# Units of last-stage weights in the mLSTM stage: a fixed step for each load and each split

## The chip, the cores and the metric

One core of one Trainium2 chip runs the whole kernel in one launch. The metric is the device time of an execution in microseconds, median over several runs. The profile is of one further execution on the chip.

## What is computed

Two decoder layers on a sequence of 2048 tokens of width 1024, each `x <- x + mixer(rmsnorm(x))`, and a last norm. The first mixer is an mLSTM (4 heads, per head 512 value and 256 key columns), the second an RG-LRU with block-diagonal gates. The reference, cut to the part in which the change lies, and to where the weights of the last stage are used:

```python
q = jnp.einsum('bshd,hde->bhse', xch, w_q).astype(jnp.float32) * (M_DK ** -0.5)
k = jnp.einsum('bshd,hde->bhse', xch, w_k).astype(jnp.float32)
v = jnp.einsum('bshd,hde->bhse', xmh, w_v).astype(jnp.float32)
...
def step(carry, inp):                       # over chunks of the sequence
    ...
    Sm = jnp.einsum('bhtk,bhsk->bhts', qb, kb) * W
    num = (decay[..., None] * jnp.einsum('bhtk,bhkv->bhtv', qb, C)
           + jnp.einsum('bhts,bhsv->bhtv', Sm, vb))
    ...
    C_new = d_last[..., None, None] * C + jnp.einsum('bhs,bhsk,bhsv->bhkv', w_last, kb, vb)
...
r = jax.nn.sigmoid(jnp.einsum('bsnc,ncd->bsnd', xb, w_a).reshape(bsz, s, R_WIDTH) + b_a)
ig = jax.nn.sigmoid(jnp.einsum('bsnc,ncd->bsnd', xb, w_x).reshape(bsz, s, R_WIDTH) + b_x)
...
return y @ w_out
```

## The kernel before

Every float32 operand of a matmul is split in two parts: `hi`, a cast to float32r on ScalarE (ACT, L759), and `lo = x - hi` on VectorE (DVE, L762). A product is three matmuls (`mm3`, L359 to L361): hi by hi, hi by lo, lo by hi. So weights cost a load, a cast and a subtraction before TensorE (PE) can use them.

The stages run one after the other: `phase_a1` (input projection), `phase_a2` (the mLSTM stage), `phase_b1` (output projection and the second layer's input projection) and `phase_b2` (gates, scan, output projection, last norm).

In `phase_a2` a loop runs over 32 blocks (h, b): 4 heads by 8 blocks of 256 tokens, each of two chunks c of 128. One pass, here a step, does the recurrence of block (h, b) and the projections of the block after it. In program order: `norm` of the block before, `loads` (xc, xm, sz, o and the rows qb and db of the next block, through the queue of SP), `recur` for chunk 0, `finish` of the block before (transposes `pt`, `y`, its write through the queue of GpSimd, POOL), `qk` (q and k of the next block), `recur` for chunk 1, `score`, and `value` for both chunks. `value` projects v and evicts it from PSUM: `vh` by ACT (L954), `vl` by DVE (L955). `recur` makes `kv` for two halves m of the state, adds it to the states `C0` and `C1` on DVE (L986) and splits these to `Ch` and `Cl`; there is one `kv` bank pair, so the second half's matmuls wait for DVE to read the first. It also makes the numerator `n`, which `hh` reads (L1009); there is one `n`, too. Mean and variance `mv` (L1017) go to POOL (`frs`, L1022 to L1025), then ACT normalizes `hh` (L1029).

The stage also prepares weights in two ways, through one pool `wraw` of two buffers:

- `head_weights` loads and splits the q, k and v weights of a head. The call for q stands in step b = 3 and that for k in b = 5 of the head before; v is called for in `qk` of a head's block 0, that is in step 7 of the head before, and has one pair of buffers.
- `later_weights` is a generator of 20 units for `phase_b2`: 8 of gate weights (128 x 768, written to `d_gw`) and 12 of output weights (128 x 1024, to `d_ow`). A unit takes both buffers: it loads `raw`, casts it to `hi` and subtracts in place, and POOL writes both parts to DRAM. Five units are called for in each head, at b = 1, 2, 4, 6 and 7.

Where an instruction ends up in its engine's queue is not decided by the place of the call: a scheduler lays the queues out, taking instructions as their inputs and buffers come free, and each engine then works through its queue in order. The method `order(first, then)` (L765) adds a constraint without a semaphore: an instruction of `then` stands behind those of `first` on the same engine. In this stage it is used for the first head only before the change (L820 to L823, L876 and L889). `split_into` (L756) returns the cast and the subtraction.

Of the kernel before, what the change touches and what calls it, by code (L numbers as in the profile page):

```python
# [7 lines left out]
F32 = mybir.dt.float32  # L8
F32R = mybir.dt.float32r
I32 = mybir.dt.int32  # L10
AF = mybir.ActivationFunctionType
ALU = mybir.AluOpType
# [9 lines left out]
H = 4  # L22
DV = 512
# [283 lines left out]
class Trunk:  # L307
# [465 lines left out]
    def phase_a2(self, wq, wk, wv, rgate, rwout, D):  # L773
        tc, nc = self.tc, self.nc
        BL = 256
        NB = T // BL
        with ExitStack() as ctx:
# [12 lines left out]
            vh = [va.tile([P, 516], F32R, name=f"vh{i}") for i in range(NVA)]  # L790
            vl = [va.tile([P, 516], F32R, name=f"vl{i}") for i in range(NVA)]
# [10 lines left out]
            def head_weights(h, names):  # L802
                w = W.setdefault(h, {})
                for nm in names:
                    src = {"q": wq[h], "k": wk[h], "v0": wv[h, :, :, 0:256], "v1": wv[h, :, :, 256:512]}[nm]
                    raw = wp.tile([P, KV, 256], F32, tag="wraw", name="wraw", bufs=2)
                    nc.sync.dma_start(raw, src)
                    if nm[0] == "v":
                        j = int(nm[1])
                        if j == 0:  # L810
                            w["v"] = (wp.tile([P, KV, 512], F32R, tag="vwh", name="vwh"),
                                      wp.tile([P, KV, 512], F32R, tag="vwl", name="vwl"))
                        hi, lo = (t[:, :, j * 256:(j + 1) * 256] for t in w["v"])
                    else:
                        pool = ob if h % 2 else wp
                        w[nm] = (pool.tile([P, KV, 256], F32R, tag=nm + "wh", name=nm + "wh"),
                                 pool.tile([P, KV, 256], F32R, tag=nm + "wl", name=nm + "wl"))
                        hi, lo = w[nm]
                    a = self.split_into(hi, lo, raw, "a", "v")
                    if h == 0 and nm[0] == "v":  # L820
                        self.order((self.kT,), a)
                    if h == 0 and nm in "qk":
                        self.order(a, self.tail[-4:])  # L823

            def later_weights():

                parts = [(rgate[i // 2, :, i % 2 * 768:(i % 2 + 1) * 768],
                          [D["gw"][i, :, l * 768:(l + 1) * 768] for l in range(2)]) for i in range(8)]
                parts += [(rwout[k], [D["ow"].rearrange("(h k) p (l n) -> k l p h n", h=2, l=2)[k, l] for l in range(2)])
                          for k in range(12)]  # L830
                for src, keep in parts:
                    n = src.shape[-1]
                    raw, hi = (wp.tile([P, KV * 256], F32, tag="wraw", name="wraw", bufs=2)[:, 0:n] for _ in range(2))
                    nc.sync.dma_start(raw, src)
                    self.split_into(hi.bitcast(F32R), raw.bitcast(F32R), raw, "a", "v")
                    for t, k in zip((hi, raw), keep):
                        nc.gpsimd.dma_start(k, t if n == 768 else t.rearrange("p (h n) -> p h n", h=2))
                    yield

            def project(h, b):  # L840
# [14 lines left out]
                def loads():  # L855
                    if (h, b) != (0, 0):
                        rows()
                    if (h, b) == (0, 0):
                        head_weights(h, ("q", "k"))
                    xm = lp.tile([P, KV, BL], F32, tag="xm", name="xm")  # L860
                    xc = lp.tile([P, KV, BL], F32, tag="xc", name="xc")
                    nc.sync.dma_start(xc, D["xc"][hs, :, bs].rearrange("k p t -> p k t"))
                    nc.sync.dma_start(xm, D["xm"][hs, :, bs].rearrange("k p t -> p k t"))
                    if (h, b) == (0, 0):
                        rows()
                    S["sz"] = sz = lp.tile([P, KV, BL], F32, tag="sz", name="sz")
                    S["o"] = o = lp.tile([P, 2, DV], F32, tag="o", name="o")
                    nc.sync.dma_start(sz, D["sz"][hs, :, bs].rearrange("k p t -> p k t"))
                    nc.sync.dma_start(o, D["o"][b * 2:b * 2 + 2, :, h * DV:(h + 1) * DV].rearrange("c p n -> p c n"))
                    for nm, x in (("xc", xc), ("xm", xm)):  # L870
                        hi = xp.tile([P, KV, BL], F32R, tag=nm + "h", name=nm + "h")
                        lo = xp.tile([P, KV, BL], F32R, tag=nm + "l", name=nm + "l")
                        fi = (h, b, nm) == (0, 0, "xc")
                        a = self.split_into(hi, lo, x, "v" if fi else "a", "v")
                        if fi:
                            self.order(a, self.tail[-4:])  # L876
                        S[nm] = (hi, lo)
                    S["xcf"] = xc
# [66 lines left out]
                def value(c):  # L945
                    xh, xl = S["xm"]
                    wh, wl = W[h]["v"]
                    ps = pr.tile([P, DV], F32, tag="r", name="pj")
                    for k in range(KV):
                        cs = slice(c * P, (c + 1) * P)  # L950
                        self.mm3(ps, xh[:, k, cs], xl[:, k, cs], wh[:, k], wl[:, k], k == 0, k == KV - 1)
                    i = (b * 2 + c) % NVA
                    p2 = ps.rearrange("p (a b) -> p a b", a=2)
                    nc.scalar.copy(halves(vh[i]), p2)  # L954
                    nc.vector.tensor_tensor(halves(vl[i]), p2, halves(vh[i]).bitcast(F32), op=ALU.subtract)  # L955

                return S, [loads, qk, score, lambda: value(0), lambda: value(1)]

# [93 lines left out]
            later = later_weights()  # L1052
# [6 lines left out]
            for i, (h, b) in enumerate(blocks):  # L1059
                if i + 1 < len(blocks):  # L1060
                    Sn, (loads, qk, score, v0, v1) = project(*blocks[i + 1])
                else:
                    Sn, loads = None, lambda: None
                    qk = score = v0 = v1 = loads
                if late:
                    norm(*late)
                loads()
                recur(h, b, 0, S)
                if late:
                    finish(*late)  # L1070
                qk()
                recur(h, b, 1, S)
                score()
                v0()
                v1()
                if b in (3, 5) and h < H - 1:
                    head_weights(h + 1, "q" if b == 3 else "k")
                elif b in (1, 2, 4, 6, 7):
                    next(later, None)
                late = (h, b, S)  # L1080
                S = Sn
            norm(*late)
# [571 lines left out]
```

## Time and profile before

| | us |
|---|---|
| median of 3 runs | 3015.86 (3013.2 to 3016.79) |
| the profiled execution | 3013.4 |
| its span, first to last instruction | 3011.5 |
| PE busy | 2868.1 (95% of the span) |
| DVE busy | 2126.0 (71%) |
| ACT busy | 1515.3 (50%) |
| POOL busy | 456.2 (15%) |
| value evictions by ACT (`vh`, L954), first and last start | 1015.4, 1726.5 |

Times in the profile's rows count from the start of the span. A row of the timeline has start, length, engine, line, operation, out<-in, shapes and, in brackets, how long the engine was idle before and what it waited for. The granted clock of PE is a share of its full speed. The value evictions mark the steps of the mLSTM stage, and the stage lasts from about 1005 to about 1745 us.

### The profile page before, as it was taken

The page shows a single profiled execution, that of the slowest core. Times are in us where ns is not written, and L with a number is a line of the kernel's source. Part 1 is how long each engine was busy: PE and PEld are TensorE (multiplying, and loading weights), DVE is VectorE, ACT ScalarE, POOL GpSimd, SP SyncE. Part 2 cuts the span into 40 slices and gives each one's busy share as a digit, 9 for nine tenths or more (in the row PEclk, how much of TensorE's full clock was granted, in tenths as well). Part 3 has the DMA queues.
Part 4 walks back from the last instruction along what each step waited for, and adds up shares of the span by engine and source line. Part 5 has one row for each costly group of instructions (what it writes and reads, how often), then busy time and mean ns, then how long its engine had stood idle before and what let it go on. Part 6 is the DMA issues. An engine that isn't in the chain of part 4 may idle for free. (4 is left out here: it accounts for less than half of the span.)

```text
span 3011.5 us, 43205 instructions
## 1 busy us (share of the span) xinstructions
PE 2868.1 (95%) x15442; PEld 2455.6 (82%) x15442; DVE 2126.0 (71%) x3584; ACT 1515.3 (50%) x2545; POOL 456.2 (15%) x846
## 2 busy tenths in 40 slices
PE   7999999999999899898998979999999999899997
PEld 5799987899987798897988968787788887678885
DVE  7766798536577587787777855677888566666763
ACT  6344555324345566566665633434434322976761
POOL 1211122102123111112112111101221111000000
PEclk9999999999999999999999989999999999999998
DMA  6767677668889754546455467776776665878855
GB/s 229 270 219 248 231 253 242 216 208 307 273 309 301 232 167 160 191 143 218 157 181 183 148 237 256 264 231 202 259 241 227 212 198 181 307 256 300 295 196 171
DMA packets 294839, 686.58 MB, mean 228 GB/s; under 512 B 29024, under 2 KB 107616, under 8 KB 294624
## 3 DMA queue, kind: packets, MB, share of 16 engines
q1 hardware_dynamic: 227440, 450.34, 47.0%
q0 software_dynamic: 66608, 232.43, 20.3%
q8 instruction: 121, 1.98, 0.3%
q10 hardware_dynamic: 576, 1.05, 0.1%
q14 instruction: 94, 0.77, 0.1%
HBM read 446.53 MB, written 237.17 MB: 227 GB/s over the span
## 5 line engine op out<-in xcount | busy, mean ns | idle before, releaser
L759 ACT CAST s<-raw 128x512 fp32r<-128x512 f32 (+1 forms) x280 | 172.1, 620 | 259.9 <-PE pd L361 69.3
L762 DVE TENSOR_TENSOR s<-raw,s 128x512 fp32r<-128x512 f32 (+1 forms) x280 | 191.6, 689 | 64.1 <-ACT s L759 63.1
L359 PE MATMUL acc<-yh,wr 128*128 128x512 f32 x384 | 151.2, 402 | 17.1 <-DMA wr<-d_ow 8.3
L360 PE MATMUL acc<-yl,wr 128*128 128x512 f32 x384 | 153.0, 398 | 0.6 <-DVE yl L762 0.6
L361 PE MATMUL acc<-yh,wr 128*128 128x512 f32 x384 | 152.6, 398 | 0.0
L759 ACT CAST u<-t 128x512 fp32r<-128x512 f32 x112 | 68.8, 619 | 154.1 <-PE pc L361 51.0
L686 DVE SCALAR_TENSOR_TENSOR xc<-xm,vec,xc 128x512 f32<-128x512 f32 x192 | 139.2, 746 | 5.8 <-ACT xc L684 4.4
L762 DVE TENSOR_TENSOR u<-t,u 128x512 fp32r<-128x512 f32 x112 | 76.7, 690 | 84.8 <-ACT u L759 84.3
L759 ACT CAST s<-sum 128x512 fp32r<-128x512 f32 (+1 forms) x120 | 74.1, 618 | 115.8 <-PE pc L361 44.3
L359 PE MATMUL pa<-u,s 128*128 128x512 f32 x304 | 122.1, 402 | 4.6 <-ACT p L258 3.1
L360 PE MATMUL pa<-u,s 128*128 128x512 f32 x304 | 121.4, 399 | 0.0
L361 PE MATMUL pa<-u,s 128*128 128x512 f32 x304 | 121.3, 400 | 0.1
L686 DVE SCALAR_TENSOR_TENSOR xc<-xr,vec,xc 128x512 f32<-128x512 f32 x144 | 106.0, 748 | 9.2 <-ACT xc L684 7.9
L986 DVE SCALAR_TENSOR_TENSOR C<-C,dl,kv 128x516 f32<-128x516 f32 x112 | 83.6, 746 | 39.8 <-PE kv L361 39.8
L759 ACT CAST Ch<-C 128x516 fp32r<-128x516 f32 x120 | 74.7, 623 | 65.9 <-DVE da L1004 52.5
L359 PEld LDWEIGHTS acc<-yh,wr 128*128 128x128 f32 x384 | 72.7, 191 | 38.1 <-issue 8.7
L359 PE MATMUL pj<-vwh,xmh 128*128 128x512 f32 x256 | 102.7, 402 | 0.3 <-ACT vwh L759 0.3
L360 PE MATMUL pj<-vwl,xmh 128*128 128x512 f32 x256 | 99.8, 390 | 0.7 <-DVE vwl L762 0.7
L762 DVE TENSOR_TENSOR s<-sum,s 128x512 fp32r<-128x512 f32 (+1 forms) x120 | 82.6, 689 | 25.0 <-ACT s L759 24.0
L361 PE MATMUL pj<-vwh,xml 128*128 128x512 f32 x256 | 100.1, 391 | 0.0
L359 PE MATMUL kv<-vh,kh 128*128 128x258 f32 x240 | 73.8, 307 | 26.4 <-ACT vh L954 15.3
L360 PE MATMUL pd<-u,s 128*128 128x512 f32 x224 | 88.5, 395 | 1.6 <-DVE u L762 1.6
(479 smaller groups left out, 10089.2 us busy)
## 6 DMA issues: line engine op xcount, KB each, us to landing
wr<-d_ow SPq DMA_DIRECT2D x96, 512.0 KB, 4.4
d_wx<-s POOLq DMA_DIRECT2D x64, 512.0 KB, 4.3
s<-d_wx SPq DMA_DIRECT2D x64, 512.0 KB, 4.4
s<-d_ws SPq DMA_DIRECT2D x64, 512.0 KB, 6.2
raw<-in_wxz_dram SPq DMA_DIRECT2D x124, 256.0 KB, 4.8
d_wr<-s POOLq DMA_DIRECT2D x48, 512.0 KB, 3.7
s<-d_wr SPq DMA_DIRECT2D x48, 512.0 KB, 4.2
wg<-d_gw SPq DMA_DIRECT2D x32, 768.0 KB, 5.0
```

Source lines behind the costliest of these rows:

```text
L359: mm(out, sh, mh, start=first, stop=False, skip_group_check=resumed)
L360: mm(out, sh, ml, start=False, stop=False, skip_group_check=resumed)
L361: mm(out, sl, mh, start=False, stop=last, skip_group_check=resumed)
L686: nc.vector.scalar_tensor_tensor(out, x[:, j:j + TB], self.v(wn, m * 4 + j), out, op0=ALU.mult, op1=ALU.add)
L759: a = nc.scalar.copy(hi, src)
L762: b = (nc.gpsimd if lo_eng == "p" else nc.vector).tensor_tensor(lo, src, hi.bitcast(F32), op=ALU.subtract)
L986: nc.vector.scalar_tensor_tensor(C2, C2, self.dl[:, r:r + 1], p2, op0=ALU.mult, op1=ALU.add)
```

## The change

Three things, all in `phase_a2`. The q and k weights of the next head are called for in steps 0 and 1 instead of 3 and 5, and their splits stand behind `self.valued`, the last value eviction (ACT behind ACT, DVE behind DVE). The units are cut in two: the load, issued from a step's start and put behind `self.loaded`, the load of `o` of that step, and the split with its writes, called for at the step's end and put behind `self.valued`. And the units have other steps: b = 2 to 6 in head 0, 2 to 5 in heads 1 and 2, 0 to 6 in head 3.

```diff
                     a = self.split_into(hi, lo, raw, "a", "v")
                     if h == 0 and nm[0] == "v":
                         self.order((self.kT,), a)
-                    if h == 0 and nm in "qk":
-                        self.order(a, self.tail[-4:])
+                    if nm in "qk":
+                        if h == 0:
+                            self.order(a, self.tail[-4:])
+                        else:
+                            self.order(self.valued, a)
...
-                    nc.sync.dma_start(raw, src)
-                    self.split_into(hi.bitcast(F32R), raw.bitcast(F32R), raw, "a", "v")
+                    self.order(self.loaded, (nc.sync.dma_start(raw, src),))
+                    yield
+                    a, v = self.split_into(hi.bitcast(F32R), raw.bitcast(F32R), raw, "a", "v")
+                    self.order(self.valued, (a, v))
                     for t, k in zip((hi, raw), keep):
                         nc.gpsimd.dma_start(k, t if n == 768 else t.rearrange("p (h n) -> p h n", h=2))
                     yield
...
-                    nc.sync.dma_start(o, D["o"][b * 2:b * 2 + 2, :, h * DV:(h + 1) * DV].rearrange("c p n -> p c n"))
+                    self.loaded = (nc.sync.dma_start(o, D["o"][b * 2:b * 2 + 2, :, h * DV:(h + 1) * DV].rearrange("c p n -> p c n")),)
...
-                    nc.scalar.copy(halves(vh[i]), p2)
-                    nc.vector.tensor_tensor(halves(vl[i]), p2, halves(vh[i]).bitcast(F32), op=ALU.subtract)
+                    self.valued = (nc.scalar.copy(halves(vh[i]), p2),
+                                   nc.vector.tensor_tensor(halves(vl[i]), p2, halves(vh[i]).bitcast(F32),
+                                                           op=ALU.subtract))
...
                 loads()
+                extra = b < 7 if h == H - 1 else 2 <= b <= 5 + (h == 0)
+                if extra:
+                    next(later, None)
                 recur(h, b, 0, S)
...
                 v1()
-                if b in (3, 5) and h < H - 1:
-                    head_weights(h + 1, "q" if b == 3 else "k")
-                elif b in (1, 2, 4, 6, 7):
+                if extra:
                     next(later, None)
+                if b < 2 and h < H - 1:
+                    head_weights(h + 1, "qk"[b])
```

The built programs show what the scheduler makes of it. The order of every engine is the same in both outside this stage. First the queue of SP in head 1 (`in_rgate` is a unit's load, `in_wq` that of q weights; the other rows are loads of a step). Before:

```order
L834 DMA wraw_12863<-in_rgate_dram 128x768
L851 DMA qb_13152<-d_q_88 128x256
L869 DMA o_12338<-d_o_80 128x2x512
L834 DMA wraw_13143<-in_rgate_dram 128x768
L863 DMA xm_12876<-d_xm_81 128x4x256
L862 DMA xc_12877<-d_xc_82 128x4x256
L868 DMA sz_12337<-d_sz_83 128x4x256
L853 DMA db_12873<-d_dec_89 128x256
L807 DMA wraw_13423<-in_wq_dram 128x1024
L834 DMA wraw_13702<-in_rgate_dram 128x768
```

and after:

```order
L874 DMA o_12886<-d_o_80 128x2x512
L837 DMA wraw_12897<-in_rgate_dram 128x768
L868 DMA xm_13441<-d_xm_81 128x4x256
L873 DMA sz_12885<-d_sz_83 128x4x256
L858 DMA db_13438<-d_dec_89 128x256
L867 DMA xc_13442<-d_xc_82 128x4x256
L856 DMA qb_13997<-d_q_88 128x256
L874 DMA o_13166<-d_o_80 128x2x512
L868 DMA xm_13721<-d_xm_81 128x4x256
L837 DMA wraw_13177<-in_rgate_dram 128x768
```

Before, four loads into `wraw` stand within one step's loads, in the first steps of the head; after, there is one to a step, behind that step's `o`, and SP's loads of a step run about one step ahead of its work.

Second, the queue of DVE at the start of a step in head 2, behind the eviction of block 4's second chunk (`C0`, `C1` are the state's halves, `y` the output of the block before). Before:

```order
L955 TENSOR_TENSOR vl3_9957<-pj_15335,vh3_9953 128x2x256
L762 TENSOR_TENSOR xml_15376<-xm_15363,xmh_15375 128x1024
L762 TENSOR_TENSOR Cl0_15389<-C0_14564,Ch0_15388 128x516
L986 SCALAR_TENSOR_TENSOR C1_14583<-C1_14583,dl_77,kv_15404 128x516
L1004 TENSOR_SCALAR da_15422<-n_15379 128x1
L1005 SCALAR_TENSOR_TENSOR da_15422<-n_15379,da_15422,enT_76 128x1
L1007 RECIPROCAL da_15422<-da_15422 128x1
L1009 SCALAR_TENSOR_TENSOR hh_15426<-n_15379,da_15422,o_15088 128x512
L762 TENSOR_TENSOR Cl1_15413<-C1_14583,Ch1_15412 128x516
L1016 BN_STATS st_15429<-hh_15426 128x6
L1046 TENSOR_TENSOR y_15432<-y_15432,skx_14956 128x1024
```

and after:

```order
L960 TENSOR_TENSOR vl3_9957<-pj_15336,vh3_9953 128x2x256
L762 TENSOR_TENSOR xml_15374<-xm_15361,xmh_15373 128x1024
L762 TENSOR_TENSOR wraw_15097<-wraw_15097,wraw_15098 128x1024
L762 TENSOR_TENSOR Cl0_15390<-C0_14557,Ch0_15389 128x516
L992 SCALAR_TENSOR_TENSOR C1_14576<-C1_14576,dl_77,kv_15405 128x516
L1010 TENSOR_SCALAR da_15423<-n_15380 128x1
L1052 TENSOR_TENSOR y_15433<-y_15433,skx_14955 128x1024
L762 TENSOR_TENSOR Cl1_15414<-C1_14576,Ch1_15413 128x516
L1011 SCALAR_TENSOR_TENSOR da_15423<-n_15380,da_15423,enT_76 128x1
L1054 TENSOR_TENSOR y_15433<-y_15433,sz_14806 128x1024
L1013 RECIPROCAL da_15423<-da_15423 128x1
L908 SCALAR_TENSOR_TENSOR qd_15484<-pj_15457,db_15358 128x512
```

A unit's subtraction now stands third in the step, behind the eviction and `xml`; in the step before the change there is no `wraw` row at all. `hh` falls behind both `y`. A few rows further, in both, comes `C0` of the second chunk and then `xcl`; the rows ahead of that `C0` are the same but for the unit's and for `mv`, which follows it after the change.

Third, ACT at the end of the stage, from the last value eviction on (`t30`, `t31` are the first loads of `phase_b1`, `u220` to `u223` their parts). Before:

```order
L954 CAST vh3_9953<-pj_18648 128x2x256
L759 CAST Ch0_18681<-C0_16771 128x516
L759 CAST u220_18855<-t30_18827 128x512
L759 CAST u221_18858<-t30_18827 128x512
L759 CAST Ch1_18705<-C1_16790 128x516
L1042 ACTIVATE y_18725<-pt_18726,vec_58 128x256
L759 CAST u223_18899<-t31_18829 128x512
L759 CAST u222_18861<-t31_18829 128x512
```

and after:

```order
L959 CAST vh3_9953<-pj_18658 128x2x256
L759 CAST wraw_18420<-wraw_18419 128x1024
L759 CAST Ch0_18688<-C0_16760 128x516
L1048 ACTIVATE y_18732<-pt_18733,vec_58 128x256 x2
L759 CAST Ch1_18712<-C1_16779 128x516
L1048 ACTIVATE y_18732<-pt_18740,vec_58 128x256 x2
L759 CAST u220_18855<-t30_18827 128x512
L759 CAST u221_18858<-t30_18827 128x512
L759 CAST u223_18899<-t31_18829 128x512
L759 CAST u222_18861<-t31_18829 128x512
L1035 ACTIVATE hh_18726<-hh_18726,frs_18778 128x512
```

The last unit's cast follows the last eviction. The tiles `t30` and `t31` lie in the memory of the two `wraw` buffers: their loads wait for that unit's writes now, where they waited for a unit written some five steps earlier. The `u` casts moved together, ahead of the last norm of `hh`.

## The prediction

> **What bounds the kernel now.** The change touches only the mLSTM stage, so I cut that stage by its steps. A step here runs from one start of the second value cast (L954, the `vh` of a block's second chunk) to the next; step (h, b) is the pass of the loop for head h and block b. First view: busy time by stretch (us from the start, its length, then PE, PEld, DVE, ACT and POOL busy with counts, the granted clock, the DMA share, GB/s). The stretches are steps (0,0) to (0,2), (0,7) to (1,2), (1,3) to (1,6), (1,7) to (2,2) and (2,7) to (3,2).
>
> ```profile
> 1019.30:1088.10 68.80, 61.98 (x430) 57.61 (x429) 55.31 (x100) 42.04 (x77) 13.22 (x27) 0.98 0.62 204
> 1172.40:1274.00 101.60, 87.45 (x583) 80.44 (x582) 75.50 (x133) 59.57 (x112) 17.99 (x34) 0.93 0.61 197
> 1274.00:1358.10 84.10, 83.58 (x615) 79.05 (x614) 69.39 (x128) 53.61 (x105) 10.21 (x24) 1.00 0.43 138
> 1358.10:1457.90 99.80, 86.36 (x584) 80.56 (x583) 76.37 (x133) 61.14 (x112) 21.29 (x34) 0.93 0.65 216
> 1542.00:1644.00 102.00, 86.96 (x579) 80.55 (x578) 75.17 (x132) 60.15 (x111) 22.57 (x36) 0.92 0.62 206
> ```
>
> In the third row PE is busy 83.58 of 84.10 us at clock 1.00: four steps of 84.10 / 4 = **21.03 us**, bound by TensorE. The four steps around each change of head take 101.60, 99.80 and 102.00 us, with 13 to 15 us of PE idle and a lower clock. Against 84.10 that is 17.5 + 15.7 + 17.9 = 51.1 us; the first three steps are 68.80 - 3 x 21.03 = 5.7 us over. So **56.8 us** of excess lie in 15 steps.
>
> The same view for the tile `wraw` alone (DVE, ACT, POOL busy) says where the splits run:
>
> ```profile
> 1172.40:1274.00 101.60, 9.83 (x9) 8.58 (x9) 6.16 (x10) 0.93 0.61 197
> 1274.00:1358.10 84.10, 0.00 (x0) 0.00 (x0) 0.00 (x0) 1.00 0.43 138
> ```
>
> All nine of that head are in the rough stretch, none in the quiet one. The waits of PE, and then of ACT, between 1019.3 and 1726.5 (total us, times, longest):
>
> ```profile
> PE pt L1039 <- ACT hh L1029: 15.5, 9, 6.4
> PE kv L359 <- ACT vh L954: 15.0, 5, 4.5
> PE kv L359 <- DVE C L986: 10.3, 11, 2.9
> ```
> ```profile
> ACT wraw L759 <- DMA wraw<-in_rwout_dram: 15.9, 6, 5.1
> ...
> ACT wraw L759 <- DMA wraw<-in_rgate_dram: 10.4, 4, 6.5
> ```
>
> PE waits for things that ACT does late, and ACT is late because it stands at a split whose weights have not landed. One such place in the timeline (start, length, in brackets the idle time before it):
>
> ```profile
> 1374.29 0.34 SPq L834 DMA_DIRECT2D wraw<-in_rwout_dram  x1
> ...
> 1379.62 1.04 ACT L759 CAST wraw<-wraw 128x1024 fp32r<-128x1024 f32 x1 [5.15 <-DMA wraw<-in_rwout_dram]
> ...
> 1383.01 1.52 ACT L1029 ACTIVATE hh<-hh,frs 128x512 f32<-128x512 f32 x2 [2.35 <-POOL frs L1025]
> ...
> 1383.88 0.48 PE L1039 MATMUL pt<-ident,hh 128*128 128x128 f32 x1 [6.36 <-ACT hh L1029]
> ```
>
> The load is issued only when the preceding unit has been written out; the cast stands at the head of ACT's queue, idle for 5.15 us, the normalization behind it, and PE loses 6.36 us.
>
> **The change part by part.** No arithmetic is added or removed: 20 unit loads, 26 splits (20 units, 3 q, 3 k) and 40 writes all stay.
>
> *The stalls that go.* By the order shown, every unit load stands a step ahead of its split, and every q, k and unit split stands behind a step's second value eviction. What is late next for the load is the preceding unit's write, since the buffers are two:
>
> ```profile
> d_ow<-wraw POOLq DMA_DIRECT2D x24, 512.0 KB, 4.2
> ...
> d_gw<-wraw POOLq DMA_DIRECT2D x16, 384.0 KB, 3.3
> ...
> wraw<-in_wv_dram SPq DMA_DIRECT2D x8, 512.0 KB, 5.1
> ...
> t<-d_y SPq DMA_DIRECT2D x4, 512.0 KB, 10.2
> ```
>
> (KB, median us to landing.) A unit split early in step n is through ACT and DVE some 4 us in, and its write has landed some 8 us in (4 + 4.2); SP, which now waits there with `sz`, `db` and `xc` queued behind, then loads for a split 13 us later, against 5.1 us for a load of that size. So I count all 56.8 us as freed, and then charge what the splits cost in their new place.
>
> *The splits in steady steps.* PE has no slack in a 21.03 us step, so the question is whether DVE has. In a quiet step that begins at 1109.4:
>
> ```profile
> 1110.60 1.22 DVE L762 TENSOR_TENSOR xml<-xm,xmh 128x1024 fp32r<-128x1024 f32 x1
> 1111.73 0.69 DVE L762 TENSOR_TENSOR Cl<-C,Ch 128x516 fp32r<-128x516 f32 x1
> ...
> 1119.04 0.74 DVE L986 SCALAR_TENSOR_TENSOR C<-C,dl,kv 128x516 f32<-128x516 f32 x1
> 1120.43 1.23 DVE L762 TENSOR_TENSOR xcl<-xc,xch 128x1024 fp32r<-128x1024 f32 x1 [0.65 <-ACT xch L759]
> ```
>
> DVE works without a break from the value eviction to the `C` at 1119.04, which frees the bank for PE's next `kv`. A split of 128x1024 takes 1111.73 - 1110.60 = 1.13 us of its queue, as `xml` does. In the order shown it stands ahead of that `C`, while one mv (0.1) moves behind: `C` comes some 1.0 us later. DVE then idled 0.65 us for `xch`, which swallows most: `xcl`, and with it the chain through the second half, POOL's `frs`, ACT's norm and the next value cast, comes at 1119.04 + 1.03 + 0.66 = 1120.73, or with mv 1120.83, against 1120.43: **0.4 us** per step. The splits stand in 7 + 6 + 6 + 7 = 26 steps, one of them the tail: 25 x 0.4 = 10.0 us. Bounds: 0 (ACT and DVE are idle later in the step and might take it up) and the full price of a split, from the one early step with three splits at full clock:
>
> ```profile
> 1040.50:1064.70 24.20, 21.30 (x153) 19.95 (x153) 19.91 (x35) 15.17 (x30) 5.65 (x11) 1.00 0.66 222
> 1064.70:1088.10 23.40, 21.64 (x147) 20.46 (x147) 18.23 (x33) 15.16 (x29) 2.79 (x7) 0.93 0.56 184
> 1172.40:1195.40 23.00, 18.10 (x126) 16.32 (x124) 17.23 (x31) 14.12 (x27) 2.93 (x7) 0.98 0.63 200
> ```
>
> (24.20 - 21.03) / 3 = 1.06 us each, or 26.5 us for 25. I take 0.4, nearer to the idle 0.65 us of the row than to a step in which a DMA was late as well.
>
> *The changes of head.* The v splits stay. For heads 2 and 3 their loads find the buffers free a step early, and I charge nothing. For head 1 the last unit of head 0 is split just ahead: 0.8 us of cast, 3.3 of write, 5.1 of load, so v lands about 10 us into step (0,7), with `qh` and `kT` queued on ACT behind its cast. That step took 23.00 us before (third row); I leave it at that: **+2.0 us** of the excess stay. Bounds 0 and 5, the latter as in the stall shown.
>
> *The tail.* The last unit now runs in the last step, and phase B's first four loads of y take over its buffers. Before they were issued long before the end, and the last norm came at 1743:
>
> ```profile
> 1716.72 2.22 SPq L1159 DMA_DIRECT2D t<-d_y  x4
> ```
> ```profile
> 1743.07 1.52 ACT L1029 ACTIVATE hh<-hh,frs 128x512 f32<-128x512 f32 x2 [9.30 <-POOL frs L1025]
> ```
>
> Now the first two wait for the unit's writes: the last value cast at 1726.5 (the edge where the last full step ends), about 0.5 for it, 1.04 of cast, 1.2 of subtraction, 4.2 of write, so about 1734. ACT splits those tiles ahead of the last norm. With 4.2 to 10.2 us of landing and two casts (1.2) ACT is free between 1739 and 1745: up to 2.3 us late. DVE gets four splits out of the chain ahead of the block's first `hh`, which gives some back. I take **+1 us**, with bounds of -2 (that gain alone) and +5 (twice the 2.3).
>
> *Sum.* 56.8 - 10.0 - 2.0 - 1.0 = 43.8 us. The profiled execution took 3013.4 us, which is 2.5 below the median of the runs, 3015.86. 3013.4 - 43.8 = 2969.6, and at the median **2972 us**.
>
> **The rivals.** (a) *The full price.* The split costs 1.06 us in every step: no other gap takes it up, because PE, which waits at `kv` for `C`, is itself full. For it: the step at 1040.50. Against: only one of its three splits stood in the full half of DVE. 56.8 - 26.5 - 3 = 27.3 us, 2988.6 at the median.
>
> (b) *Hidden.* DVE is idle some 3 us late in a quiet step (69.39 / 4 = 17.3 of 21.03 busy), and the scheduler's order leaves room: the splits cost nothing. 56.8 - 3 = 53.8, 2962.
>
> (c) *The wait comes back.* Loads still land late because SP stands at a write or behind `o`, and half of the excess stays: 56.8 / 2 - 3 = 25.4 less, and with it half of the 10.0, 20.4: 2995. For it: SP is one queue, and every unit load waits for a write now. Against: the 13 us worked out above.
>
> (d) *Slower.* Every one of the 25 steps gets a stall of its own at `kv`, in one piece, and the clock falls after each. The row that shows it:
>
> ```profile
> 1066.68 0.39 PE L359 MATMUL kv<-vh,kh 128*128 128x258 f32 x1 [1.76 <-DVE C L986]
> ```
>
> That step, 1064.70 to 1088.10 above, ran at a mean clock of 0.93 and took 23.40 us, 2.4 over. 25 x 2.4 = 60: 56.8 - 60 - 3 = -6.2 us, 3022. It decides from (56.8 - 3) / 25 = 2.15 us a step on. Against: a split delays `C` by 1.0 us, not 1.76, and the step at 1040.50, with 24.20 - 21.30 = 2.9 us of PE idle in several pieces, kept 1.00. [...]
>
> **How the numbers follow.** Forecast (2965 to 2980) 0.52, (a) 0.22, (b) 0.10, (c) 0.07, (d) 0.09. The range is to hold 8 in 10: 2958 to 2994 reaches past (b) and (a) and nearly to (c), and leaves (d) and a part of (c) out. A measurement of this kernel can tell about 0.2%, 6 us, from no change. Faster by more than that: all but (d) and a little of (c), 0.88. Within: 0.04, between (c) and (d). Slower: 0.08, most of (d).
>
> **What would show it.** In the profile of the changed kernel: `wraw` splits one to a step, each right behind the second `vh` cast, in every stretch; no wait of ACT for `wraw` over 1 us but at v of head 1; PE's waits for `hh` and `vh` almost gone, and in their place many short ones for `C` at `kv`, or for `hh` at `n`, of 0.3 to 1 us; quiet steps of 21.3 to 21.5 us instead of 21.03, at clock 1.00; steps around the changes of head near 21; the last norm within 3 us of its old distance from the last value cast. Steps of 22 and more at clock 1.00 would mean (a), the same with clock below 0.95 (d), a cast of `wraw` that waits several us (c). A tail longer by more than 5 us would make my third charge wrong, and a stage B that starts differently would be outside what I worked out.

## The result, and the profile after

| | before | after |
|---|---|---|
| median of the runs measured together | 3014.53 us | 2962.78 us (2962.53 to 2963.57) |
| the profiled execution, its span | 3013.4, 3011.5 | 2962.7, 2960.7 |
| ratio | 1 | 0.9829, 95% interval 0.9812 to 0.9846 |

The change saves 51.8 us, 1.7%. The prediction was 2972 in 2958 to 2994: right in its direction and range, 9 us too slow.

First the busy time by stretch of the changed kernel, cut at the same casts as before (columns as in the prediction). The rows are the whole of steps (0,0) to (3,6), then (0,3) to (0,6), (0,7) with (1,0), (1,7) with (2,0), (2,1) with (2,2), (2,3) to (2,6), (2,7) with (3,0), and the end of the stage.

```profile
1020.70:1671.80 651.10, 637.84 (x4600) 598.91 (x4598) 556.06 (x1007) 434.15 (x818) 102.79 (x221) 1.00 0.56 182
1081.90:1167.10 85.20, 83.51 (x611) 78.81 (x610) 73.31 (x133) 56.53 (x110) 14.70 (x32) 1.00 0.59 192
1167.10:1212.10 45.00, 41.30 (x285) 38.05 (x284) 35.20 (x64) 28.29 (x54) 6.23 (x14) 0.96 0.57 193
1339.40:1379.20 39.80, 39.27 (x283) 36.75 (x282) 33.86 (x63) 27.61 (x53) 5.12 (x12) 1.00 0.54 172
1379.20:1421.50 42.30, 41.90 (x305) 39.40 (x305) 36.54 (x67) 28.80 (x55) 5.12 (x12) 1.00 0.48 150
1421.50:1506.10 84.60, 83.81 (x611) 79.08 (x611) 73.34 (x133) 57.52 (x110) 16.10 (x32) 1.00 0.68 218
1506.10:1545.90 39.80, 39.21 (x283) 36.59 (x282) 33.83 (x63) 27.59 (x53) 5.12 (x12) 1.00 0.50 159
1671.80:1710.00 38.20, 23.17 (x109) 18.74 (x110) 22.70 (x38) 15.94 (x30) 12.30 (x19) 0.73 0.92 341
```

The 31 steps take 651.1 us; before, they took 1726.5 - 1019.3 = 707.2. Nothing rough is left but the third row. A step with a gate unit takes 85.20 / 4 = 21.30 us, one with an output unit 84.60 / 4 = 21.15, one with a q or k split 42.30 / 2 = 21.15, against 21.03 without a split before. And the pairs (1,7) with (2,0) and (2,7) with (3,0) take 39.80, 19.9 a step: they have 283 matmuls where two other steps have 305. The first chunk of a head has no state to multiply with q, and the last one makes no new state.

The splits now (the tile `wraw` alone: DVE, ACT, POOL), from (0,7) to (1,2) and from (1,3) to (1,6):

```profile
1167.10:1254.40 87.30, 5.84 (x5) 5.02 (x5) 1.18 (x2) 0.98 0.52 171
1254.40:1339.40 85.00, 4.09 (x4) 3.55 (x4) 5.05 (x8) 1.00 0.64 205
```

Five (two of them v) and four in four steps each, where there were nine and none. The waits of PE, and of ACT for `wraw` loads, in the 31 steps:

```profile
PE kv L359 <- DVE C L992: 8.0, 24, 1.7
PE pt L1045 <- ACT hh L1035: 2.2, 2, 1.8
```
```profile
ACT vwh L759 <- DMA wraw<-in_wv_dram: 1.9, 2, 1.2
```

PE's waits for ACT's `hh` fell from 15.5 to 2.2 us, those for `vh` (15.0) are gone from the list, and ACT waits for a `wraw` load at v only. The waits for `C` were 11 before, with 10.3 us in all; now they are 24 with 8.0 us, one of 1.7 in step (0,0) and the others of 0.2 to 0.5.

The two spans differ by 50.9 us before rounding. The steps give 56.1 of it; the first value cast comes 1.4 later; and the time from the last value cast to the end went from 1285.1 to 1288.9 us, 3.8 more.

### The profile page after: what moved, and what is told of

The parts are those of the page before. It is cut to its first block, busy times and chain, and to the rows that moved or that the text cites. A ratio compares the mean times of both kernels' runs of the same rounds, so it can differ in the third digit from the quotient of the medians.

```text
span 2960.7 us, 43267 instructions
## 1 busy us (share of the span) xinstructions
PE 2850.7 (96%) x15442; PEld 2440.3 (82%) x15442; DVE 2124.2 (72%) x3584; ACT 1516.8 (51%) x2545; POOL 445.8 (15%) x846
## 3 DMA queue, kind: packets, MB, share of 16 engines
q0 software_dynamic: 66608, 232.43, 20.9%
## 4 chain that ended last, share of the span: by engine, by line
PE 35%; DVE 12%; issue 6%; ACT 4%; DMA 1%; POOL 1%; SPq 0%; DVEq 0%; POOLq 0%; ACTq 0%
PE pa L361 2%; PE pa L359 2%; PE pa L360 2%; PE pd L360 2%; PE pd L359 2%; PE pd L361 2%; PE pc L359 2%; PE pc L360 2%; PE pc L361 2%; PE acc L360 2%; PE acc L361 2%; PE acc L359 2%; DVE Cl L762 2%; PE pb L360 1%; PE pb L361 1%
## 5 line engine op out<-in xcount | busy, mean ns | idle before, releaser
L360 PE MATMUL pd<-u,s 128*128 128x512 f32 x224 | 88.6, 395 | 1.3 <-DVE u L762 1.3
L359 PE MATMUL pd<-u,s 128*128 128x512 f32 x224 | 88.3, 394 | 0.0
```

The source lines that it names most:

```text
L359: mm(out, sh, mh, start=first, stop=False, skip_group_check=resumed)
L360: mm(out, sh, ml, start=False, stop=False, skip_group_check=resumed)
```

## Where a split's price arises

In the changed kernel, DVE at the start of a step with a q or k split (2,2), whose value cast starts at 1400.37:

```profile
1401.59 1.22 DVE L762 TENSOR_TENSOR xml<-xm,xmh 128x1024 fp32r<-128x1024 f32 x1
1402.72 1.22 DVE L762 TENSOR_TENSOR kwl<-wraw,kwh 128x1024 fp32r<-128x1024 f32 x1
...
1405.13 0.15 DVE L1010 TENSOR_SCALAR da<-n 128x1 f32<-128x1 f32 x1
1405.20 1.21 DVE L1052 TENSOR_TENSOR y<-y,skx 128x1024 f32<-128x1024 f32 x1
...
1411.58 1.20 DVE L762 TENSOR_TENSOR xcl<-xc,xch 128x1024 fp32r<-128x1024 f32 x1
```

From `xml` to `xcl` it is 1411.58 - 1401.59 = 9.99 us. In the prediction's quiet step it was 1120.43 - 1110.60 = 9.83, of which 0.65 idle for `xch`: with a split of 1.14 us the queue lost its idle time and grew by 0.16, and the step grew by 0.12. So the chain is the one that the prediction wrote down: value eviction, DVE's queue to `C` and `xcl`, then the second half, `mv`, POOL's `frs`, ACT's norm, the next value cast. The prediction's 0.4 came out as 0.16 because the small `da` operations no longer stand behind one another. In the quiet step of before, on DVE:

```profile
1113.00 0.15 DVE L1004 TENSOR_SCALAR da<-n 128x1 f32<-128x1 f32 x1
...
1113.63 0.75 DVE L1009 SCALAR_TENSOR_TENSOR hh<-n,da,o 128x512 f32<-128x512 f32 x1
```

Three operations on one column each took 0.63 us of the queue: the second, the third and `hh` each read the result of the one ahead and start 0.03 to 0.04 us behind its end, where `Cl` starts 0.09 ahead of the end of `xml` (1111.73 against 1110.60 + 1.22). After, `y` stands behind the first `da`, 0.07 us from its start, and others behind the next two: the three take 0.27, which is 0.36 less. A gate unit's split of 768 columns is shorter, 0.87 us of the queue, and yet its step is 0.28 longer, not less. From the value cast to `xcl` it is 1120.43 - 1109.38 = 11.05 us in the quiet step, 11.21 in (2,2) and 1093.20 - 1081.87 = 11.33 in (0,3), a step with a gate unit: the difference lies in this part of the queue. Its rows there have small gaps: the subtraction stands right behind `vl` and begins 0.13 us late, at 1083.21, when its own cast on ACT has ended (1083.18); two `da` still stand behind one another; and `mv`, which stays ahead of `C`, stands right behind the operation whose result it reads and begins 0.19 us late.

## The experiments

Times of whole programs differ by some microseconds for other reasons: over the profiled executions here the first value cast comes between 1019.3 and 1027.4 us, and from the first `pa` matmul of phase B to the last instruction of an engine, whose code is the same in all, it takes between 1259.9 and 1268.1. So beside the median stand two terms read from the profile: the 31 steps, and the end of the stage (last value cast to the first `pa` matmul of phase B). The ratio is against runs of before on the same chip.

| run | median us | ratio, 95% interval | steps us | end us |
|---|---|---|---|---|
| the change | 2962.78 | 0.9829 (0.9812 to 0.9846) | 651.1 | 23.8 |
| e1_no_sub | 2960.71 | 0.9817 (0.9801 to 0.9834) | 644.9 | 23.7 |
| e2_double_sub | 2987.50 | 0.9908 (0.9893 to 0.9923) | 667.0 | 31.9 |
| e3_value_first | 2970.78 | 0.9848 (0.9832 to 0.9864) | 658.4 | 23.3 |
| e4_other_steps | 2963.03 | 0.9826 (0.9812 to 0.9841) | 654.8 | 21.2 |
| e5_qk_only | 3011.51 | 0.9984 (0.9974 to 0.9993) | 700.4 | 20.7 |
| e6_units_only | 2977.26 | 0.9877 (0.9862 to 0.9891) | 666.7 | 23.3 |
| e7_no_split_order | 2970.41 | 0.9855 (0.9840 to 0.9870) | 656.1 | 20.9 |
| e8_load_not_ordered | 2966.91 | 0.9845 (0.9831 to 0.9860) | 653.1 | 23.4 |
| e9_qk_together | 2961.08 | 0.9818 (0.9797 to 0.9840) | 650.2 | 21.2 |
| e10_split_late | 2971.90 | 0.9854 (0.9835 to 0.9873) | 655.6 | 26.4 |
| e11_together_late | 2964.07 | 0.9829 (0.9809 to 0.9848) | 657.0 | 20.9 |
| e12_after_frs | 2959.32 | 0.9808 (0.9795 to 0.9822) | 649.2 | 20.3 |

In the kernel before the steps take 707.2 and the end 21.2.

### Which part of the change does it (e5 to e8)

Only the q and k part:

```diff
-                    self.order(self.loaded, (nc.sync.dma_start(raw, src),))
-                    yield
+                    nc.sync.dma_start(raw, src)
...
-                    self.order(self.valued, (a, v))
...
-                extra = b < 7 if h == H - 1 else 2 <= b <= 5 + (h == 0)
-                if extra:
-                    next(later, None)
+                extra = b in (1, 2, 4, 6, 7)
                 recur(h, b, 0, S)
```

> Only the q and k part of the change: their steps 0 and 1 and their order behind the value eviction; units as before (whole, no order, b = 1, 2, 4, 6, 7). In the built order the units still crowd into steps 7, 1, 2 and 3 of a head. If the wait of ACT at a unit's cast is the cause, over half of the excess stays: 2963 + 30 = 2993 (2985 to 3003), with waits of several us of ACT for wraw loads. Rival (q and k, hoisted to the change of head, were the cause): 2965 to 2970.

3011.51: 4.5 us less than the 3016.01 of before beside it. The waits of PE and of ACT in its steps:

```profile
PE pt L1043 <- ACT hh L1033: 30.0, 16, 6.6
```
```profile
ACT wraw L759 <- DMA wraw<-in_rwout_dram: 12.6, 5, 5.4
```

ACT still stands at the units' casts, and PE at `hh` behind it. The cause was the units, more so than expected. The other half alone, with q and k called for at 3 and 5 and free:

> Only the units' part: loads and splits in fixed steps; q and k are called for at b = 3 and 5 as before and without order. In the built order q and k stand in the second third of steps (h,4) and (h,6), behind xch, with their loads issued ahead. If units were the cause: 2963 to 2968, no wait of ACT for wraw over 1 us but at v. Rival (q and k): 2985 or more.

2977.26, 38.8 less than before: between the two forecasts. Now ACT stands at q and k, three times each:

```profile
ACT kwh L759 <- DMA wraw<-in_wk_dram: 5.7, 3, 2.8
ACT qwh L759 <- DMA wraw<-in_wq_dram: 4.6, 3, 2.2
```

Their loads go into the two buffers that a unit has just left, in the same steps. Part by part it is 4.5 and 38.8, together 51.8: either part left alone goes on stalling ACT. Then the two kinds of order, each left out of the whole change:

```diff
-                    self.order(self.valued, (a, v))
```

(and the same for q and k)

> The change without its order of splits (units, q and k): loads of units stay behind o, steps stay. In the built order units keep their steps all the same, since their loads are fixed; q and k go up into the change of head, right behind v. If the place of the loads does the work: 2963 to 2970, the rest from q and k at the change of head. Rival (the order behind the value eviction does it): 2985 to 3000.

```diff
-                    self.order(self.loaded, (nc.sync.dma_start(raw, src),))
                     yield
+                    nc.sync.dma_start(raw, src)
```

> The change without its order of loads: a unit's load is called for beside its split, with no constraint; splits stay behind the value eviction. In the built order of SP the loads stand nearly where they stood. If the split's place does the work: 2961 to 2965. Rival (the early load does it): ACT waits 2 us and more at each of 20 casts: 3000.

Steps of 656.1 and 653.1 us, 5.0 and 2.0 more than with both. Either order alone keeps the units one to a step in the built program, and the other end follows it; so neither of the two is needed for that, and both together are worth little more than one. What the new steps and the earlier call would do without either order is not known: no run leaves out both. (The profiled execution of e8 took 2971.98 us, 9.3 more than that of the change, and 6.7 of it lie ahead of the first value cast.)

### What a split costs (e1 to e3)

```diff
-                    a, v = self.split_into(hi.bitcast(F32R), raw.bitcast(F32R), raw, "a", "v")
-                    self.order(self.valued, (a, v))
+                    a = nc.scalar.copy(hi.bitcast(F32R), raw)
+                    self.order(self.valued, (a,))
```

> Leaves out the units' subtraction on DVE (the raw weights are written as the second part); load, cast, order and writes stay. Theory L (the price of a split is the lateness of C at kv less a slack of some 0.7 us that PE had): steps with a unit fall from 21.14 and 21.30 to 21.0, the waits of kv for C vanish, 8 x 0.28 + 11 x 0.12 = 3.6 us less: 2959. Theory X (the prediction's 0.4 us a split): 20 x 0.4 = 8 us less: 2955. Theory D (loads and writes beside the work cost the time, not DVE's queue): no change, 2963.

By stretch, steps (0,3) to (0,6), (2,1) with (2,2), and (2,3) to (2,6):

```profile
1082.10:1166.20 84.10, 83.84 (x616) 79.47 (x615) 69.62 (x129) 56.42 (x110) 14.68 (x32) 1.00 0.59 195
1375.20:1417.50 42.30, 41.89 (x306) 39.42 (x305) 36.54 (x67) 28.76 (x56) 5.85 (x13) 1.00 0.48 163
1417.50:1501.60 84.10, 83.80 (x616) 79.43 (x615) 69.58 (x129) 57.16 (x110) 15.38 (x31) 1.00 0.66 213
```

Steps with a unit are back at 84.10 / 4 = 21.03; the q and k steps, whose splits are whole, stay at 21.15. So the price is DVE's queue, 0.28 us for a gate unit and 0.12 for an output unit, and not the transfers, which are all there. It is 0.4 nowhere; in the short step (3,6) it is 0.8 (20.21 against 19.41). (The median fell by 2.1 only, for phase B took 3.6 us longer in it.) Next, more of the same:

```diff
+                    v2 = nc.vector.tensor_tensor(raw.bitcast(F32R), raw, hi, op=ALU.subtract)
-                    self.order(self.valued, (a, v))
+                    self.order(self.valued, (a, v, v2))
```

> Subtracts hi a second time from every unit, behind the same value eviction, so that DVE's queue is another 1.14 us (0.9 for gate weights) longer ahead of C. L and X: the slack is used up, so nearly all of it comes through: 19 unit steps of 22.1 to 22.4 us, 2963 + 19 = 2982, at clock 1.00. Rival b (DVE's idle time late in the step takes it up): under 4 us more, 2966. Rival d (a stall of over 1 us in one piece pulls the clock down): clock 0.93 in these steps and 2.4 us more for each beside the 1.0: 2963 + 19 x 3.4 = 3028.

The same stretches, (0,3) to (0,6) and (2,3) to (2,6):

```profile
1084.50:1170.30 85.80, 83.42 (x611) 78.82 (x610) 75.66 (x137) 55.26 (x109) 14.69 (x32) 1.00 0.58 191
1431.00:1517.80 86.80, 84.64 (x612) 79.31 (x611) 76.90 (x137) 56.20 (x109) 16.08 (x32) 1.00 0.66 213
```

Neither L nor X: on average 0.15 us more a step for 0.87 of gate subtraction, 0.55 for 1.14 of output subtraction; of the total's 24.7 the pairs (h,7) with (h+1,0) take 9.5 (48.72, 41.85 and 43.67 us) and the end 8.1. The rows of ACT show what may have paid for the rest:

```profile
1125.88 1.52 ACT L1036 ACTIVATE hh<-hh,frs 128x512 f32<-128x512 f32 x2 [2.03 <-POOL frs L1032]
1127.31 0.56 ACT L960 CAST vh<-pj 128x512 fp32r<-128x512 f32 x1
1127.78 0.84 ACT L759 CAST wraw<-wraw 128x768 fp32r<-128x768 f32 x1
1128.51 1.06 ACT L759 CAST xmh<-xm 128x1024 fp32r<-128x1024 f32 x1
```

The scheduler put `xmh`, which had stood ahead of the value cast, behind it, 1.0 us out of the chain. That this is what paid is argued, not shown. Rival d is out: the clock is 1.00 in both rows, with 85.80 - 83.42 = 2.4 and 2.2 us of PE idle in four steps. And e3 asked for that order of ACT alone, on the changed kernel:

```diff
+                        if nm == "xm" and (h, b) != (0, 0):
+                            self.order(self.valued[:1], a[:1])
```

> The cast of the next xm stands behind the second value cast on ACT instead of ahead of it, so that the value cast comes 0.9 us sooner after the last matmul of v. L: the slack of the loop grows from 0.7 to 1.6 us, more than the 0.95 us of a split: no wait of kv for C, steps of 20.95 to 21.05 with and without a unit, 4 us less: 2959. X (the chain behind C through xcl sets the price): xml and xcl do not come sooner, steps stay at 21.14 and 21.30: 2963, or 1 to 3 us more where xml, now later, is missed.

```profile
1424.40:1509.10 84.70, 83.59 (x611) 78.90 (x610) 73.29 (x132) 57.43 (x110) 16.09 (x32) 1.00 0.66 218
```
```profile
PE kv L359 <- DVE C L994: 11.4, 25, 2.6
```

Steps of 21.18 as in the changed kernel (21.15), and 8.0 us more in all, most of it in the first two steps of heads 2 and 3. What L forecast did not come: the waits of `kv` for `C` did not go, there are 25 of them. But the order of DVE changed too: it now takes the first `C` of a step behind `vl`, where it stood ahead of it, and PE waits at that `kv`, a gain on ACT that the new order of DVE gave away. So e3 does not decide between L and X.

### Another place in the step (e10 to e12)

If the chain is value cast, DVE, `mv`, `frs`, norm, value cast, a split behind `mv` should be free:

```diff
-                    self.order(self.valued, (a, v))
+                    self.order((self.kh,), (a,))
+                    self.order(self.valued, (v,))
...
                 v0()
+                if extra:
+                    next(later, None)
                 v1()
-                if extra:
-                    next(later, None)
```

> The units' split stands elsewhere in the step, otherwise the change as it is: cast behind the first kh on ACT, which idles there for 1.4 us, subtraction behind the eviction of the first chunk's v on DVE, which idles there for 1.7 us before C, both behind mv and so off the chain mv, frs, norm, value cast. Theory X (a unit costs what it adds to DVE's queue between the value eviction and mv): unit steps 21.02 instead of 21.14 and 21.30, 3.6 us less; step (0,7) 2 us less and the end of the stage 1 to 2 less, since each write ends 6 us sooner: 2956. Rival L (the wait of kv for C, wherever the split stands) and D (DMA): unit steps stay at 21.14 and 21.30: 2960 to 2963.

Steps (2,3) to (2,6), and then POOL at the end of step (2,4), and DVE and ACT beside it:

```profile
1425.60:1511.70 86.10, 83.91 (x616) 79.40 (x615) 73.11 (x132) 55.66 (x108) 17.76 (x32) 1.00 0.66 209
```
```profile
1465.86 0.81 POOL L1034 TENSOR_TENSOR frs<-frs 128x2 f32<-128x2 f32 x1
```
```profile
1465.41 1.22 DVE L762 TENSOR_TENSOR wraw<-wraw 128x1024 fp32r<-128x1024 f32 x1
```
```profile
1466.71 1.52 ACT L1038 ACTIVATE hh<-hh,frs 128x512 f32<-128x512 f32 x2 [1.79 <-POOL frs L1034]
```

All forecasts fell: the three steps with a unit take 21.6 to 21.8 us, longer than in the change ((2,6) has none here and takes 21.03). But the reason speaks for X. POOL's last `frs`, an operation on 128x2 that takes 0.19 us elsewhere, took 0.81 and ended at 1466.67, just behind DVE's subtraction (1466.63); the norm, which waits for it, came 0.6 us later, and the step is 0.6 longer (21.64 against 21.03). In this execution the subtraction was running 15 times when the last `frs` began, and that `frs` took 0.51 to 0.99 us; the other 17 took 0.19 or 0.20, ten of them beside `kl`, another operation of DVE. So `frs` took longer beside the subtraction and nowhere else; what holds it up there, no run shows.

So the subtraction was made to wait for that `frs`, with the units' writes behind it too; q and k stay in steps 0 and 1, and the units have other steps, b = 1 to 5, in head 3 0 to 4:

```diff
+                    self.order((self.kh,), (a,))
+                    self.order(self.valued, (v,))
+                    self.tc.add_manual_dep(v.ins, self.frs.ins.name, mybir.DependencyInfo(
+                        mybir.DependencyClass.Sync, mybir.DependencyReason.DATA), reason="frs")
...
-                extra = b < 7 if h == H - 1 else 2 <= b <= 5 + (h == 0)
+                extra = b < 5 if h == H - 1 else 1 <= b <= 5
```

> [...] In the run with the late split the last frs took 0.51 to 0.99 us wherever the subtraction ran beside it, 0.19 elsewhere, and unit steps took 21.64 us. Theory X (the step is the chain value cast, DVE, mv, frs, norm, value cast): the last frs takes 0.19 again and the unit steps of head 3 fall from 21.64 to 21.02; with steps (h,7) and (h,0) at 19.9 and the end of the stage as before the change, 2963 - 3.6 - 5 - 3.4 = 2951. Rival (the late place itself costs, by ACT's cast or by the wait of kv for C): unit steps of 21.3 to 21.7, 2960 or more.

Steps (3,2) to (3,5), and DVE and POOL late in step (3,3):

```profile
1569.10:1653.40 84.30, 83.44 (x611) 78.72 (x610) 72.88 (x131) 55.44 (x107) 13.39 (x28) 1.00 0.54 184
```
```profile
1608.96 1.23 DVE L762 TENSOR_TENSOR wraw<-wraw 128x1024 fp32r<-128x1024 f32 x1 [0.60 <-POOL frs L1036]
```
```profile
1608.73 0.19 POOL L1036 TENSOR_TENSOR frs<-frs 128x2 f32<-128x2 f32 x1
```

Each of the 32 last `frs` takes 0.19 again, and steps (3,3) to (3,5) take 21.02, with a unit's subtraction in two of them, (3,3) among them. (The first of the four, 21.25, waits for `C`.) Of the 13 steps that split a unit alone (without the short (3,0)), eight take 21.01 to 21.04: there X holds, not L, by which the place would not matter, and the subtraction has a place that costs nothing. The other five take 21.25 to 21.64; three of these stand right behind the steps in which k comes late, and what lengthens them no run isolates. The time, 2959.32 us, is the lowest median of the study; but the intervals of its ratio (0.9795 to 0.9822) and of the change's (0.9812 to 0.9846) overlap, so by the medians it isn't shown to be faster. By the two terms it is 1.9 + 3.5 = 5.4 us shorter. It fell 8 short of the 2951 expected: in steps (0,2), (1,2) and (2,2), where k and a unit are split, ACT waits 1.2 to 2.5 us for the load of k, and these steps take 21.8 to 23.4 us.

### Step (0,7) and the end of the stage (e4, e9, e11)

In the changed kernel, SP and ACT in step (0,7), which begins at 1167.1:

```profile
1171.56 2.21 SPq L807 DMA_DIRECT2D wraw<-in_wv_dram  x2
```
```profile
1176.72 1.05 ACT L759 CAST vwh<-wraw 128x1024 fp32r<-128x1024 f32 x1 [1.24 <-DMA wraw<-in_wv_dram]
...
1179.44 1.04 ACT L759 CAST vwh<-wraw 128x1024 fp32r<-128x1024 f32 x1 [0.67 <-DMA wraw<-in_wv_dram]
```

The v load goes out when the writes of the unit have landed, for which SP waits 1.0 us at most, and v is there 9.6 and 12.3 us into the step, about the 10 of the prediction. And at the end of the stage, DVE:

```profile
1683.21 1.29 DVE L762 TENSOR_TENSOR u<-t,u 128x512 fp32r<-128x512 f32 x2
1687.97 1.29 DVE L762 TENSOR_TENSOR u<-t,u 128x512 fp32r<-128x512 f32 x2 [3.46 <-ACT u L759]
1689.18 0.17 DVE L1023 BATCH_NORM_AGGREGATE mv<-st 128x2 f32<-128x6 f32 x1
```

`mv`, which the last norm needs, stands behind the splits of phase B's first tiles; their loads were let go by the last unit's write, for which SP waited 17.0 us. Two runs took the units away from both places:

```diff
-                extra = b < 7 if h == H - 1 else 2 <= b <= 5 + (h == 0)
+                extra = b < 5 if h == H - 1 else 1 <= b <= 5
...
-                if b < 2 and h < H - 1:
-                    head_weights(h + 1, "qk"[b])
+                if b in (0, 6) and h < H - 1:
+                    head_weights(h + 1, "q" if b == 0 else "k")
```

> Same constraints, other steps: q at b = 0, units at b = 1 to 5 (head 3: 0 to 4), k at b = 6. No unit stands ahead of the v loads and none in the last two steps. If the 3 us of step (0,7) are the wait of v's load for a unit's write, the step falls from 24.1 to 21 to 22; if the longer end of the stage is the wait of the first loads of phase B for the last unit's write, the last norm comes 16 us after the last value cast instead of 19.1. Sum: -2.5 - 3 + 1 (a split more in two steps (h,7)): 2958. Rival: v's load now waits for k's split in three heads: 3 us in each, 2963 - 3 + 6 = 2966.

The end is 21.2 us again, as before the change, so the 2.5 us are the last unit's. But the rival is right as well: v now waits behind k in three heads, and the pairs (h,7) with (h+1,0) take 44.75, 42.73 and 41.31 us. With q and k together in step 0:

> Other steps: q and k of the next head both split in step 0, units at b = 1 to 5 (head 3: 0 to 4), so that no split stands ahead of the v loads in step (h,7) and none in the last two steps. If (0,7) and (1,0) were long for v's load (24.07 and 20.97, where others have 19.9), they fall by 5 us; the end of the stage is 2.6 + 0.8 us shorter, as in the run with k at b = 6; two splits in each of three steps cost 0.6 us there. Sum -5 - 3.4 + 1.8: 2956. Rival (two splits behind one another make a stall that pulls the clock down, or v is late anyway): 2963 or more.

```profile
1169.50:1209.40 39.90, 39.27 (x283) 36.65 (x282) 33.91 (x63) 27.67 (x54) 5.07 (x12) 1.00 0.52 172
1209.40:1254.00 44.60, 43.67 (x319) 40.99 (x318) 37.57 (x68) 29.21 (x57) 6.76 (x14) 1.00 0.50 166
```

(0,7) with (1,0) takes 39.90 instead of 45.00: the 5 us are v's. The next two steps of head 1 take 44.60 - 42.30 = 2.3 more, and the same in head 0; but they hold 319 matmuls against 305, so a part of that is work that moved over the steps' edge, and the step behind them is 0.6 shorter (20.68 against 21.30). Both measures with the late split, which does not wait for `frs` here:

> Both: q and k together in step 0, units at b = 1 to 5 (head 3: 0 to 4) with their split in the late place. Theory X: 20 units free of charge, steps (h,7) and (h,0) at 19.9, end of the stage as before the change: 2956 - 3.4 = 2953. Rival: the gains are the same microseconds counted twice, 2956.

2964.07: its steps with a unit take 21.4 to 21.7, much as in e10, and (0,2), (1,2) and (2,2) take 22.1 to 23.1, which eats up what the ends give.

## Why the prediction came out as it did

- **The stalls that go: right.** All the excess went but that of (0,7), and the cause was the one named: e5 shows it by its absence. But it was measured against 21.03 us for every step, and that is the step that failed: the pairs around the later heads need 39.80, not 42.06, and step (0,0), with casts at 1020.7 and 1039.6, 18.9. The four short steps give 4.5 us, (0,0) 2.1: **6.6 us more** than the 56.8. The matmul counts of the stretch stood in the prediction's own row for (0,7), 126 against 615 / 4 = 154, and were read as nothing.
- **0.4 us a split: the chain right, the size wrong.** Measured 0.28 in 7 whole steps with a gate unit, 0.12 in 10 with an output unit and in 6 with q or k: 2.0 + 1.2 + 0.7 = 3.9, and 0.8 in the last full step, 20.2 after 19.4: **4.7 in place of 10.0**, counting (0,7) apart. I added the split's duration to the queue and didn't look whether the order shown fills the gaps between the `da` rows: it does, for 0.36 us.
- **Step (0,7): right in kind.** I charged 2.0 against 21.03 a step; (0,7) and (1,0) together are 45.00 - 42.06 = 2.9 over.
- **The end: right that it costs, short in size.** +1 was forecast, 2.5 measured, in the bounds of -2 to 5; and it is DVE's `mv` behind the subtractions, not ACT's norm behind the casts, that made it late.
- **Sum.** 43.8 + 6.6 + 5.3 - 0.9 - 1.5 = 53.3; the first value cast came 1.4 later, and phase B took 1.3 more: 50.6, against 50.9 of the spans.
- **The rivals.** (b) gave the right time, 2962, for a wrong reason: the splits are not hidden (e1). (a) is refuted by the steps of 21.15 and 21.30, (c) by ACT's list of waits. (d) is refuted by the clock of 1.00 over the steps with their 24 small stalls, and in e2 with 0.5 to 0.6 us of idle a step.

## What to carry to other kernels

An instruction that waits for a load should stand in an in-order queue only where the load has surely landed; a scheduler that moves it up "when the buffer is free" puts the wait ahead of everything behind it (before the change, 5.15 us of ACT at one cast, and 6.36 of PE behind it). Fixing either the load or its consumer in a step of its own ended that here (e7 and e8), with waits of ACT of 1.3 us at most left at a unit. What work costs in a full queue is read from the loop that closes the step (here value cast, DVE, `mv`, `frs`, norm, value cast), less the gaps that the new order fills; a place off that loop is free only if the work slows no engine on it, as the subtraction did in e10, where `frs` took 0.51 to 0.99 us beside it and 0.19 elsewhere. And a step's floor should be counted from its own work: steps at the edges of a loop can be shorter than the quiet ones between, here 19.9 us against 21.03.

## What the hardware showed beside that

POOL's 0.19 us operation that took up to 0.99 us beside DVE's subtraction in e10 is told above. The other is the clock after a stall. Two waits of PE in the changed kernel, and the windows behind the first and around the second:

```profile
1029.82 0.39 PE L359 MATMUL kv<-vh,kh 128*128 128x258 f32 x1 [1.68 <-DVE C L992]
...
1190.60 0.34 PE L1045 MATMUL pt<-ident,hh 128*128 128x128 f32 x1 [1.84 <-ACT hh L1035]
```
```profile
1030.00:1034.00 4.00, 4.00 (x30) 3.78 (x30) 3.96 (x9) 2.13 (x6) 0.00 (x0) 1.00 0.00 2
...
1187.37:1190.78 3.41, 1.57 (x13) 1.32 (x11) 0.70 (x1) 1.05 (x2) 1.72 (x5) 1.00 0.11 43
1190.78:1194.19 3.41, 3.05 (x15) 2.89 (x15) 2.40 (x5) 3.07 (x6) 0.00 (x0) 0.50 0.00 0
```

Full clock behind the wait of 1.68 us, half the clock behind that of 1.84. A longer wait in e3 kept the full clock:

```profile
1022.27 0.39 PE L359 MATMUL kv<-vh,kh 128*128 128x258 f32 x1 [2.70 <-DVE C L992]
```
```profile
1017.99:1021.40 3.41, 1.58 (x14) 1.38 (x12) 0.47 (x1) 1.67 (x4) 0.41 (x1) 1.00 0.86 316
1021.40:1024.81 3.41, 2.54 (x21) 2.54 (x22) 3.38 (x7) 1.28 (x3) 0.32 (x1) 1.00 0.45 157
```

So the length of one wait does not decide here. In the mLSTM stage of every profile here the clock is halved for 3.41 us or a multiple of it (in the steps of before nine times, for 3.41 to 10.24 us), and within one profile all these pieces begin on one grid of 3.41 us; the windows above are cut on that grid (in e3 by its own). Over the steps of all 14 profiles that gives 2671 pieces at full clock. In 32 of them PE was idle for 1.84 us or more in sum, and half the clock followed every one; in 2632 it was idle for 1.68 us or less, and it followed none; in the seven between it followed three, among them the 1.76 us of the prediction's row. Before and the changed kernel alone have 380 of the pieces: 1.84 us or more in nine, all followed; 1.68 or less in 369, none followed; 1.70 was not followed, 1.76 was. The edge in these profiles thus lies between 1.68 and 1.84 us, about half of such a piece, in one wait or in several (in before, 1.59 and 0.34 us in one piece were enough). The 2.70 us of e3 lay across two pieces, with 1.83 and 0.87 us idle, and a step with a unit, at some 0.2 to 0.5 us of waiting, stays far below it.
